# Gated linear attention's projection in three chunks of 512 columns instead of four of 384

## The chip, the core and the metric

The kernel runs on one core of a Trainium2 chip, as one program. TensorE (PE in the profile) multiplies matrices, VectorE (DVE), ScalarE (ACT) and GpSimd (POOL) work element by element, and SyncE (SP) issues nearly all DMA. Each engine takes its own instructions in order and waits on semaphores for the others. The metric is the device time of the whole program in microseconds (us), the median of several executions.

## What is computed

One layer of a decoder for 2048 prompt rows and 64 sample rows, in float32, cut to what the change is about:

```python
h = rms_norm(x, g_mix_pre)
proj = jnp.einsum('btd,de->bte', h, w_in)          # 1024 -> 512+128+128 | 256+256+512+512 | 16
q, k, v, gq, gk, gv, gr, glr = jnp.split(proj, points, axis=-1)
attn = swa_banded(rope(q), rope(k), v, sinks)       # window of 128, 8 heads
log_a = log_sigmoid(glr @ w_gk2 + b_gk) / 16
o, s_new = gla_chunked(gq, gk, gv, log_a, s_init)   # gated linear attention, 4 heads
gla_out = rms_norm(o, g_gla) * silu(gr)
mix = jnp.einsum('bte,ed->btd', concatenate([attn, gla_out]), w_out)
x = x + rms_norm(mix, g_mix_post)
# then a squared-ReLU MLP of width 4096 between two norms, and the residual
```

## The kernel before

Rows are cut into 17 tiles of 128 (tile 16, `NB`, holds the 64 sample rows). A float32 product is made of three: operands are split into a high part, rounded to float32r, and the rest, and `three` products (high by high, high by rest, rest by high) are summed in PSUM. A contraction over 1024 has 8 steps `k` of 128, so one tile by one chunk of columns takes 24 matmuls; for the sample rows, whose high and rest parts lie side by side as 128 rows, it takes 16.

The program has four parts: the attention (0 to some 290 us in the trace), the gated linear attention (to some 680 us), the output projection (to some 860 us) and the MLP.

The columns gq, gk, gv, gr (1536 of them) are the projection that is changed. `G_N` is the width of a chunk: four chunks of 384 columns. `projecting` multiplies one tile by a chunk into a PSUM bank of kind "a" (there are two), and then ScalarE copies the sum into `gp` (`gp_s` for the sample rows), scaled by the row's norm. These matmuls, `gproj` in the profile, are not made at one place: they are a generator, `fill`, from which other work takes a given number at a time while its own operands come from other engines. In the attention `A_FILL` says how many products are taken at which point of a unit, in the gated linear attention `G_FILL` does (34, 14, 16, 8 and 20 for each tile, 92 in all of the 96 that a tile needs). So PE has something to do while DVE and ACT make the next decays, keys and gates.

The weights of the chunks come from `w_in` by DMA (`load_gw`, tile `wg_raw`), are multiplied by the norm's gain and split (`split_gw`). The early ones (chunks 0 and 1) are loaded two a tile from tile 3 on and split by GpSimd and ACT, the late ones (chunks 2 and 3) after the attention's own weights `wa` are released, four in flight, split by ACT and DVE (`split_some`). Tiles 0 and 1 take their early chunks in the attention's last two tiles and the late ones in the part for the sample rows' attention. Then `products` projects the sample rows and tiles 2 to 15, one tile after the other.

When the last tile (15) is done with a chunk, the place of that chunk's weights is free. `load_wo` puts output weights there (`wo`; the split halves had been written to DRAM as `wo_d`), `place_mix` the first rows to be projected (`mt`), and `out_projecting` starts right behind the last `gproj`, still in the same `fill`. The order of PE, ACT and DVE in the attention is the order in which the code calls them (`InOrder`); elsewhere a scheduler orders the instructions, and it also orders SP's DMAs.

Of the kernel before, what the change touches and what calls it, by code (L numbers as in the profile page):

```python
# [21 lines left out]
P = 128  # L22
D = 1024
# [16 lines left out]
G_N = 384  # L40
# [15 lines left out]
G_EARLY, G_LATE = (0, 1), (2, 3)  # L56
# [16 lines left out]
G_GAINED = ((0, 2),)  # L73
G_NEXT = (NB, *range(2, NB))
G_ORDER = (0, 1, 2, 3)
# [3 lines left out]
WO_PARTS = ((), (0, 1, 2), (3, 4, 5), (6, 7))  # L79
# [73 lines left out]
def hybrid_step_kernel(ctx: ExitStack, tc: tile.TileContext, I, O):  # L153
# [83 lines left out]
    def load_raw(stg, k, c0, n, name, tag="w_raw", bufs=2):  # L237
# [13 lines left out]
    gw = {}  # L251

    def open_gw(chunks):
        p_ = open_pool(f"g_w{chunks[0]}", "right")
        for c in chunks:
            gw[c] = (p_, *(p_.tile([P, KT, G_N], F32R, tag=f"w{c}{u}", name=f"wg{c}_{u}") for u in range(2)))
        return p_
# [373 lines left out]
    def projecting(i, xT, chunks, act=nc.scalar):  # L631

        n, waiting = rows(i), []
        for c in chunks:
# [1764 lines left out]
```

## Time and profile before

| | |
|---|---|
| time, three runs | 2166.4, 2166.55 and 2170.19 us, median 2166.55 |
| span of the profiled execution | 2163.2 us, first to last instruction |
| instructions in it | 34238, of them 11799 matmuls |
| PE, ACT, DVE, POOL busy | 99%, 56%, 71%, 12% of the span |
| chain that ended last | PE 96%, DMA 1%, DVE 1%, ACT 1% |

The median is 3.35 us above the profiled span; this part lies around the first and the last instruction, and the change does not touch it. A matmul's end is modelled in this profile, and matmuls overlap: a PE that is busy all the time is not one that works at its peak, and the mean duration of a matmul is longer than the distance from one start to the next. Rates are therefore read from the chain and from starts in the timeline.

### The profile page before, as it was taken

The page shows a single profiled execution, that of the slowest core. Times are in us where ns is not written, and L with a number is a line of the kernel's source. Part 1 is how long each engine was busy: PE and PEld are TensorE (multiplying, and loading weights), DVE is VectorE, ACT ScalarE, POOL GpSimd, SP SyncE. Part 2 cuts the span into 40 slices and gives each one's busy share as a digit, 9 for nine tenths or more (in the row PEclk, how much of TensorE's full clock was granted, in tenths as well). Part 3 has the DMA queues.
Part 4 walks back from the last instruction along what each step waited for, and adds up shares of the span by engine and source line. Part 5 has one row for each costly group of instructions (what it writes and reads, how often), then busy time and mean ns, then how long its engine had stood idle before and what let it go on. Part 6 is the DMA issues. An engine that isn't in the chain of part 4 may idle for free.

```text
span 2163.2 us, 34238 instructions
## 1 busy us (share of the span) xinstructions
PE 2150.4 (99%) x11799; PEld 1864.7 (86%) x11799; DVE 1528.9 (71%) x3203; ACT 1220.9 (56%) x2625; POOL 258.5 (12%) x417
## 2 busy tenths in 40 slices
PE   9999999999999999999999999999999999999998
PEld 9999999999998888888888888887888888788887
DVE  7999868777875666988887555557766666555566
ACT  7999867566664444655555544344444445444454
POOL 4676501111111100000000000000000000000000
PEclk9999999999999999999999999999999999999999
DMA  7444241233437567777786777758544443766685
GB/s 242 159 142 149 98 117 46 75 108 123 147 124 276 188 217 227 250 259 273 259 275 219 261 244 223 230 181 266 177 170 161 151 160 125 247 203 195 195 262 186
DMA packets 241322, 411.54 MB, mean 190 GB/s; under 512 B 24876, under 2 KB 143132, under 8 KB 237036
## 3 DMA queue, kind: packets, MB, share of 16 engines
q1 hardware_dynamic: 240988, 409.08, 57.0%
q8 instruction: 93, 1.52, 0.3%
q14 instruction: 81, 0.66, 0.1%
q10 hardware_dynamic: 160, 0.27, 0.0%
HBM read 265.82 MB, written 143.99 MB: 189 GB/s over the span
## 4 chain that ended last, share of the span: by engine, by line
PE 96%; DMA 1%; DVE 1%; ACT 1%; issue 0%; DVEq 0%; SPq 0%; ACTq 0%
PE dn L142 26%; PE gproj L142 13%; PE uc L142 8%; PE uX L142 8%; PE out L1419 7%; PE proj L142 6%; PE ud L142 4%; PE ue L142 4%; PE ub L142 4%; PE sam L142 2%; PE dsam L142 1%; PE sc L142 1%; PE pT L142 1%; PE o L142 1%; PE av L142 1%; PE out L142 1%
## 5 line engine op out<-in xcount | busy, mean ns | idle before, releaser
L142 PE MATMUL dn<-o1t,o0s 128*128 128x512 f32 x892 | 348.2, 390 | 3.8 <-DVE o1t L229 3.8
L142 PE MATMUL dn<-o0t,o1s 128*128 128x512 f32 x892 | 347.8, 390 | 0.0
L142 PE MATMUL dn<-o0t,o0s 128*128 128x512 f32 x892 | 347.4, 389 | 0.3 <-DVE f L2071 0.3
L229 DVE TENSOR_TENSOR o1s<-rs,o0s 128x512 fp32r<-128x512 f32 x224 | 154.5, 691 | 223.0 <-ACT o0s L228 218.8
L228 ACT ACTIVATE o0s<-rs 128x512 fp32r<-128x512 f32 x224 | 141.2, 631 | 297.0 <-PE dn L142 262.0
L142 PE MATMUL gproj<-wg,gxh 128*128 128x384 f32 x1024 | 272.9, 342 | 0.0
L142 PEld LDWEIGHTS dn<-o1t,o0s 128*128 128x128 f32 x892 | 167.4, 188 | 41.1 <-DVE o1t L229 5.7
L142 PEld LDWEIGHTS dn<-o0t,o0s 128*128 128x128 f32 x892 | 167.5, 188 | 37.0 <-DVE f L2071 0.7
L142 ACT ACTIVATE st<-st 128x512 f32<-128x512 f32 x224 | 141.1, 630 | 100.3 <-DVE st L142 95.3
L142 PEld LDWEIGHTS dn<-o0t,o1s 128*128 128x128 f32 x892 | 167.4, 188 | 35.1
L142 PEld LDWEIGHTS gproj<-wg,gxh 128*128 128x128 f32 x1024 | 183.9, 188 | 3.5 <-issue 3.1
L142 PE MATMUL uc<-H,s 128*128 128x512 f32 x768 | 186.5, 391 | 0.0
L142 PE MATMUL gproj<-wg,gxl 128*128 128x384 f32 x576 | 185.8, 340 | 0.0
L142 PE MATMUL uX<-H,w 128*128 128x512 f32 x768 | 185.2, 390 | 0.0
L142 PEld LDWEIGHTS uX<-H,w 128*128 128x128 f32 x768 | 144.0, 188 | 30.3
L142 PEld LDWEIGHTS uc<-H,s 128*128 128x128 f32 x768 | 143.0, 188 | 30.6 <-ACT st L142 0.2
L1419 PE MATMUL out<-wo,mt 128*128 128x512 f32 x680 | 158.6, 392 | 0.0
L218 POOL TENSOR_TENSOR frs<-rs_v,half 128x1 f32<-128x1 f32 (+1 forms) x13 | 11.9, 925 | 1201.8 <-DVE rs_v L216 1201.8
L229 DVE TENSOR_TENSOR o1t<-rt,o0t 128x512 fp32r<-128x512 f32 x223 | 152.3, 685 | 3.8 <-ACT o0t L228 3.7
L1419 PEld LDWEIGHTS out<-wo,mt 128*128 128x128 f32 x680 | 126.5, 188 | 26.1
L228 ACT ACTIVATE o0t<-rt 128x512 fp32r<-128x512 f32 x223 | 137.8, 618 | 7.6 <-DMA rt<-t_d 4.9
L142 DVE TENSOR_TENSOR st<-st 128x512 f32<-128x512 f32 x160 | 110.7, 692 | 29.5 <-ACT st L142 25.2
(429 smaller groups left out, 4307.7 us busy)
## 6 DMA issues: line engine op xcount, KB each, us to landing
s_d<-st SPq DMA_DIRECT2D x32, 1792.0 KB, 8.5
rs<-s_d SPq DMA_DIRECT2D x224, 256.0 KB, 3.0
raw<-in_w_up SPq DMA_DIRECT2D x64, 512.0 KB, 4.6
rt<-t_d SPq DMA_DIRECT2D x128, 256.0 KB, 4.2
rt<-in_w_down SPq DMA_DIRECT2D x96, 256.0 KB, 3.2
t<-in_w_down SPq DMA_DIRECT2D x64, 256.0 KB, 3.7
t_d<-t SPq DMA_DIRECT2D x32, 512.0 KB, 5.7
h_d<-ht SPq DMA_DIRECT2D x8, 1280.0 KB, 7.6
```

What stands on the lines that cost most here:

```text
L142: ins = call(*a, **k)
L218: return nc.gpsimd.tensor_tensor(out, v[:n], e, op=ALU.pow)
L228: nc.scalar.activation(hi, src, AF.Copy)
L229: vector.tensor_tensor(lo, src, f32(hi), op=ALU.subtract)
L1419: te.matmul(banks[c], x, w[:, c * 512 : (c + 1) * 512], start=k + u == 0, stop=k == KT - 1 and u == len(products) - 1,)
```

## The change

The 1536 columns become three chunks of 512: chunk 0 is gq and gk, chunk 1 gv, chunk 2 gr. One tile by one chunk is still 24 matmuls. They are taken in the order 0, 2, 1 (`G_ORDER`). `fill` is now drawn by `pour`, in which a matmul of 512 columns counts as 4/3, so that the numbers of `A_FILL` and `G_FILL` mean the same columns as before.

Weights are kept in five pieces by chunk and step: chunk 0 in steps 0 to 5 and 6 to 7, chunk 1 in two halves, chunk 2 whole. Early are 12 pieces of 128x512 (chunk 0 and half of chunk 1), one a tile through one `w_raw` buffer instead of two a tile through two; late are the other 12, three in flight. Tiles 0 and 1 stop in the middle of chunk 1's sum and go on when the late half is there, so both "a" banks are held over that time. Output weights 0 to 3 take chunk 2's place, 4 and 5 that of chunk 1's first half, 6 and 7 that of its second; the first `mt` tiles and the gains lie in chunk 0's place.

```diff
-G_N = 384
+G_N = 512
...
-G_EARLY, G_LATE = (0, 1), (2, 3)
+G_EARLY, G_LATE = ((0, 0, 6), (0, 6, 8), (1, 0, 4)), ((1, 4, 8), (2, 0, 8))
...
+EARLY_WEIGHTS, LATE_WEIGHTS = ([(c, k) for c, k0, k1 in parts for k in range(k0, k1)] for parts in (G_EARLY, G_LATE))
...
-G_ORDER = (0, 1, 2, 3)
+G_ORDER = (0, 2, 1)
...
-WO_PARTS = ((), (0, 1, 2), (3, 4, 5), (6, 7))
+WO_PARTS = {(2, 0, KT): (0, 1, 2, 3), (1, 0, 4): (4, 5), (1, 4, KT): (6, 7)}
...
-    def load_raw(stg, k, c0, n, name, tag="w_raw", bufs=2):
+    def load_raw(stg, k, c0, n, name, tag="w_raw", bufs=1):
...
+    def open_gw(parts):
+        p_ = open_pool(f"g_w{parts[0][0]}", "right")
+        for c, k0, k1 in parts:
+            gw[c, k0] = p_
+            for u in range(2):
+                t = p_.tile([P, k1 - k0, G_N], F32R, tag=f"w{c}{k0}{u}", name=f"wg{c}{k0}_{u}")
+                gw_tiles[c, k0, u] = t
+                for k in range(k0, k1):
+                    wg[c, k, u] = t[:, k - k0, :]
         return p_
...
     def split_gw(c, k, raw):
-        if c in G_LATE or (c, k) in G_GAINED:
-            split_gained(gw[c][1][:, k, :], gw[c][2][:, k, :], raw, k)
+        hi, lo = (wg[c, k, u] for u in range(2))
+        if (c, k) in LATE_WEIGHTS or (c, k) in G_GAINED:
+            split_gained(hi, lo, raw, k)
             return
         with tc.issue_after(powers[3].ins):
             nc.gpsimd.tensor_tensor(raw, raw, gcol[:, k : k + 1].to_broadcast([P, G_N]), op=ALU.mult)
-        ac.activation(gw[c][1][:, k, :], raw, AF.Copy)
-        nc.gpsimd.tensor_tensor(gw[c][2][:, k, :], raw, f32(gw[c][1][:, k, :]), op=ALU.subtract)
+        ac.activation(hi, raw, AF.Copy)
+        nc.gpsimd.tensor_tensor(lo, raw, f32(hi), op=ALU.subtract)
...
-    def projecting(i, xT, chunks, act=nc.scalar):
-
-        n, waiting = rows(i), []
-        for c in chunks:
-            p_ = bank([P, 512], "a", f"gproj_{i}_{c}")
-            _, wh, wl = gw[c]
-            products = ((xT[1], wh), (xT[1], wl)) if i == NB else ((xT[0], wh), (xT[0], wl), (xT[1], wh))
-            for k in range(KT):
+    late_copies_g, g_banks = [], {}
+
+    def projecting(i, xT, pieces, act=nc.scalar):
+
+        n = rows(i)
+        for c, k0, k1 in pieces:
+            if k0 == 0:
+                g_banks[i, c] = bank([P, 512], "a", f"gproj_{i}_{c}")
+            p_ = g_banks[i, c]
+            for k in range(k0, k1):
+                wh, wl = (wg[c, k, u] for u in range(2))
+                products = ((xT[1], wh), (xT[1], wl)) if i == NB else ((xT[0], wh), (xT[0], wl), (xT[1], wh))
                 for u, (x, w) in enumerate(products):
-                    te.matmul(
-                        p_[:, :G_N], x[:, k, :], w[:, k, :],
-                        start=k + u == 0, stop=k == KT - 1 and u == len(products) - 1,
-                    )
-                    yield
-                    if waiting and (k, u) == (0, 2):
-                        act.activation(*waiting.pop(), scale=rstd_all[:n, i : i + 1])
+                    te.matmul(p_, x[:, k, :], w, start=k + u == 0, stop=k == KT - 1 and u == len(products) - 1)
+                    yield 4 / 3
+                    if late_copies_g and (k, u) == (0, 2):
+                        late_copies_g.pop()()
+            if k1 < KT:
+                continue
             if i not in gps:
                 gps[i] = gp_pool.tile([P, G_W], F32, tag="gp", name=f"gp_{i}", bufs=2)
             out = gps[i][:n, c * G_N : (c + 1) * G_N]
-            src = folded(out, p_[:, :G_N]) if i == NB else p_[:, :G_N]
-            if act is ac and (i, c) == (0, chunks[0]):
-                waiting.append((out, src, AF.Copy))
+            src = folded(out, p_) if i == NB else p_
+            copy = partial(act.activation, out, src, AF.Copy, scale=rstd_all[:n, i : i + 1])
+            if act is ac and (i, c) == (0, 0):
+                late_copies_g.append(copy)
             else:
-                act.activation(out, src, AF.Copy, scale=rstd_all[:n, i : i + 1])
+                copy()
...
+    def pour(n):
+
+        poured[0] += n
+        while poured[0] > 0.5:
+            cost = next(fill, 0)
+            if cost == 0:
+                break
+            poured[0] -= cost or 1
...
-            for n in range(4):
-                stage = ("w_raw", 2) if n % 2 else ("x", 2)
+            for n in range(3):
+                stage = ("w_raw", 1) if n == 1 else ("x", 2)
                 weights.append((*load_gw(*late.popleft(), *stage), stage))
         elif i >= 3:
             with tc.issue_after(third.ins):
-                for _ in range(min(2, len(early))):
+                if early:
                     weights.append((*load_gw(*early.popleft()), None))
...
-            fill = chain(fill, projecting(t, gxTs[t], G_EARLY, ac))
+            fill = chain(fill, projecting(t, gxTs[t], [(0, 0, KT)], ac))
+            if t:
+                fill = chain(fill, *(projecting(a, gxTs[a], [(1, 0, 4)], ac) for a in G_FIRST))
...
-                split_some(2)
+                split_some(1)
...
-    fill = chain(fill, *(projecting(t, gxTs[t], G_LATE, ac) for t in G_FIRST))
+    fill = chain(fill, *(projecting(t, gxTs[t], [part], ac) for part in G_LATE for t in G_FIRST))
...
-        split_some(4)
+        split_some(3)
...
-    def load_wo(ks, c):
-
-        parts = [gw[c][0].tile([P, 3, D], F32R, tag=f"w{c}{u}", name=f"wo{u}_{c}") for u in range(2)]
-        if len(ks) == 2:
-            late_mix.extend(t[:, 2, :512].rearrange("p (h t) -> p h t", h=4) for t in parts)
-            g_mix.extend(f32(t[:, 2, 512:]) for t in parts)
+    def place_late():
+
+        parts = [gw[0, 6].tile([P, 2, 512], F32R, tag=f"w06{u}", name=f"late{u}") for u in range(2)]
+        late_mix.extend(t[:, 0].rearrange("p (h t) -> p h t", h=4) for t in parts)
+        g_mix.extend(f32(t[:, 1]) for t in parts)
+
+    def load_wo(c, k0, ks):
+
+        parts = [gw[c, k0].tile([P, len(ks), D], F32R, tag=f"w{c}{k0}{u}", name=f"wo{u}_{c}{k0}") for u in range(2)]
         wo.update((k, [t[:, n, :] for t in parts]) for n, k in enumerate(ks))
         load_wo_half(ks, 0)
...
-            for c, ks in zip(G_ORDER, WO_PARTS):
-                columns = projecting(i, xT[i], (c,))
-                if after is None and c == G_ORDER[2]:
-                    yield from islice(columns, 10)
+            if after is not None:
+                yield from projecting(i, xT[i], [(c, 0, KT) for c in G_ORDER])
+                continue
+            for c, k0, k1 in ((0, 0, KT), *WO_PARTS):
+                columns = projecting(i, xT[i], [(c, k0, k1)])
+                if c == G_ORDER[1]:
+                    yield from islice(columns, 4)
+                    placed = [place_mix(j) for j in B_ORDER[:2]]
+                    place_late()
+                    yield from islice(columns, 15)
                     mixes.update((m[0], split_mix(*m, put)) for m in placed)
                 yield from columns
-                if after is None:
-                    load_wo(ks, c)
-                    if c == G_ORDER[1]:
-                        placed = [place_mix(j) for j in B_ORDER[:2]]
-                    if c == G_ORDER[3]:
-                        load_wo_half(range(KT), 1)
-                        for h, t in enumerate(g_mix):
-                            loaded = nc.sync.dma_start(t, gain_d[h : h + 1].rearrange("a d -> (a d)").partition_broadcast(P))
-                        raw = ss.tile([P, KT, P], F32, tag="part1", name="mt_raw", bufs=2)
-                        i = B_ORDER[2]
-                        with tc.issue_after(loaded.ins):
-                            nc.sync.dma_start(raw, mix_d[i])
+                if c:
+                    load_wo(c, k0, WO_PARTS[c, k0, k1])
+            load_wo_half(range(KT), 1)
+            for h, t in enumerate(g_mix):
+                loaded = nc.sync.dma_start(t, gain_d[h : h + 1].rearrange("a d -> (a d)").partition_broadcast(P))
+            raw = ss.tile([P, KT, P], F32, tag="part1", name="mt_raw", bufs=2)
+            i = B_ORDER[2]
+            with tc.issue_after(loaded.ins):
+                nc.sync.dma_start(raw, mix_d[i])
```

On PE, near the end of the projection (tile 15; `gproj_2` and the like are sums of a chunk, `wg` its weights, `gxh` and `gxl` the rows' high part and rest, `o` and `gqk` belong to the gated linear attention), before:

```order
L142 MATMUL o_9152<-S_4976,qd_4991 128x128
L142 MATMUL o_9152<-gp_8765,AT 128x128
L142 MATMUL gqk_9175<-ident,gp_9026 128x128 x4
L142 MATMUL gproj_2_9079<-wg_1_4412,gxh_8674 128x384
L142 MATMUL gproj_2_9079<-wg_0_4411,gxl_8675 128x384
L142 MATMUL gproj_3_9194<-wg_0_4413,gxh_8674 128x384
L142 MATMUL gproj_3_9194<-wg_1_4414,gxh_8674 128x384
L142 MATMUL gproj_3_9194<-wg_0_4413,gxl_8675 128x384
```

and with the change:

```order
L144 MATMUL o_8693<-S_4900,qd_4915 128x128
L144 MATMUL o_8693<-gp_8354,AT 128x128
L144 MATMUL gqk_8716<-ident,gp_8589 128x128 x4
L144 MATMUL gproj_1_8687<-wg_0_192,gxl_8257 128x512
L144 MATMUL gproj_1_8687<-wg_0_192,gxh_8256 128x512
L144 MATMUL gproj_1_8687<-wg_1_193,gxh_8256 128x512
```

Behind `gqk` chunk 3 of 24 matmuls was still to come, and two of chunk 2; now 19 matmuls of chunk 1 are, and chunk 2, whose place takes output weights 0 to 3, has ended ahead of `o`.

On SP, the loads of the first mixed rows (`mt`), of the output weights (`wo`, by `u` and chunk; `wo_d0` is step 0) and of the gains (`gain_d`), before:

```order
L1205 DMA mix_d13_76<-mo0_4986 128x512
L1379 DMA mt_4_9077<-mix_d4_67 128x1024
L1379 DMA mt_0_9075<-mix_d0_63 128x1024
L1461 DMA wo1_1_9068<-wo_d0_147 128x512
L1461 DMA wo0_1_9067<-wo_d0_147 128x512
L1461 DMA wo0_1_9067<-wo_d1_148 128x512
L1461 DMA wo1_1_9068<-wo_d1_148 128x512
L1461 DMA wo0_1_9067<-wo_d2_149 128x512
L1461 DMA wo1_1_9068<-wo_d2_149 128x512
L1461 DMA wo0_1_9067<-wo_d0_147 128x512
L1461 DMA wo1_1_9068<-wo_d0_147 128x512
L1461 DMA wo0_1_9067<-wo_d1_148 128x512
```

and with the change:

```order
L1230 DMA mix_d13_76<-mo0_4910 128x512
L1403 DMA mt_4_8598<-mix_d4_67 128x1024
L1403 DMA mt_0_8596<-mix_d0_63 128x1024
L1512 DMA late0_8600<-gain_d_158 128x512
L1512 DMA late1_8601<-gain_d_158 128x512
L1516 DMA mt_raw_8774<-mix_d1_64 128x1024
L1488 DMA wo1_20_8678<-wo_d0_147 128x512
L1488 DMA wo0_20_8677<-wo_d0_147 128x512
L1488 DMA wo0_20_8677<-wo_d1_148 128x512
L1488 DMA wo1_20_8678<-wo_d1_148 128x512
L1488 DMA wo0_20_8677<-wo_d2_149 128x512
L1488 DMA wo1_20_8678<-wo_d2_149 128x512
```

The gains and the third tile's rows (`mt_raw`) stood behind all 32 loads of `wo` and now stand ahead of them, and the second halves of steps 0 to 2 (the 7th to 12th load of `wo`) now come behind all 16 first halves.

## Rows read from the trace of the kernel before

**Rows 1.** Page, part 1: busy us (share of the span) xinstructions of each engine.

```profile
PE 2150.4 (99%) x11799; PEld 1864.7 (86%) x11799; DVE 1528.9 (71%) x3203; ACT 1220.9 (56%) x2625; POOL 258.5 (12%) x417
```

**Rows 2.** PE waits, 27 to 660 us: us in total, times, longest.

```profile
PE pT L142 <- DVE s L142: 0.4, 1, 0.4
PE pT L142 <- ACT s L142: 0.2, 1, 0.2
```

**Rows 3.** Groups of instructions by line and shape, whole span.

```profile
L142 PE MATMUL gproj<-wg,gxh 128*128 128x384 f32 x1024 | 272.9, 342 | 0.0
...
L142 PE MATMUL gproj<-wg,gxl 128*128 128x384 f32 x576 | 185.8, 340 | 0.0
```

**Rows 4.** Chain that ended last, 500 to 700 us: start us, us, what.

```profile
632.53 5.90 PE gproj L142 x34
639.05 5.26 PE gproj L142 x30
648.12 3.67 PE gproj L142 x20
...
660.83 6.86 PE out L142 x30
671.98 4.75 PE out L142 x20
...
685.80 11.84 PE out L1419 x52
```

**Rows 5.** Timeline of PE around the last tile: start us, us, what.

```profile
644.28 0.60 PE L142 MATMUL gproj<-wg,gxh 128*128 128x384 f32 x2
...
645.85 0.45 PE L142 MATMUL gl<-XQ,kt 128*64 128x64 f32 x8
...
651.63 0.38 PE L142 MATMUL o<-S,qd 128*128 128x128 f32 x2
...
653.77 0.42 PE L142 MATMUL gproj<-wg,gxh 128*128 128x384 f32 x1
...
658.37 2.02 PE L142 MATMUL out<-wo,mt 128*128 128x512 f32 x8
...
667.66 2.11 PE L142 MATMUL out<-wo,mt 128*128 128x512 f32 x8
669.70 0.45 PE L142 MATMUL gl<-XQ,kt 128*64 128x64 f32 x8
```

**Rows 6.** Stretches in the attention: busy us (instructions) of each engine, clock, DMA.

```profile
130.00:180.00 50.00, 50.00 (x347) 48.81 (x346) 45.62 (x155) 46.42 (x125) 37.30 (x63) 1.00 0.41 139
180.00:230.00 50.00, 50.00 (x344) 48.92 (x343) 45.73 (x157) 44.85 (x122) 28.06 (x54) 1.00 0.41 142
```

**Rows 7.** Tile wg_raw: ns min/median/max of its instructions; landing of its loads.

```profile
L267 POOL TENSOR_TENSOR wg_raw<-wg_raw,gcol x15: 826/827/828, 49.8 to 183.5; 128x384 f32<-128x384 f32 x15
L142 ACT ACTIVATE wg<-wg_raw x15: 507/512/527, 81.1 to 193.8; 128x384 fp32r<-128x384 f32 x15
...
DMA to landing us min/median/max: 2.4/2.4/3.3
```

**Rows 8.** Groups by line and shape, 250 to 660 us: copies out of PSUM.

```profile
L654 ACT ACTIVATE gp<-gproj,rstd_all 128x384 f32<-128x384 f32 x56 | 32.2, 574 | 11.4 <-PE gproj L142 10.7
```

**Rows 9.** Stretches around 375 us (columns as in rows 6).

```profile
370.00:375.00 5.00, 5.00 (x37) 4.66 (x36) 4.07 (x13) 3.80 (x12) 1.04 (x1) 1.00 0.00 1
375.00:380.00 5.00, 5.00 (x71) 4.54 (x70) 2.61 (x6) 1.71 (x6) 0.00 (x0) 0.66 0.51 178
```

**Rows 10.** Timeline of the DMA queue on SP, 640 to 690 us.

```profile
641.04 0.80 SPq L1379 DMA_DIRECT2D mt<-mix_d  x2
645.43 22.81 SPq L1461 DMA_DIRECT2D wo<-wo_d  x32
```

**Rows 11.** Tile wo: its loads from issue to landing.

```profile
DMA to landing us min/median/max: 5.3/6.1/6.8
```

**Rows 12.** All waits from 260 to 320 us: us in total, times, longest.

```profile
DVE mo_s L142 <- DMA wg_raw<-in_w_in: 1.1, 1, 1.1
```

More of the change, by code (lines that the diff above doesn't have):

```diff
@@ L2 @@
 from contextlib import ExitStack, nullcontext
+from functools import partial
 from itertools import chain, cycle, islice
@@ L249, in hybrid_step_kernel @@
     gcol = cpool.tile([P, KT], F32, name="gcol")
-    gw = {}
-    def open_gw(chunks):
-        p_ = open_pool(f"g_w{chunks[0]}", "right")
-        for c in chunks:
-            gw[c] = (p_, *(p_.tile([P, KT, G_N], F32R, tag=f"w{c}{u}", name=f"wg{c}_{u}") for u in range(2)))
+    gw, gw_tiles, wg = {}, {}, {}
+    def open_gw(parts):
[7 more added lines that the diff above has]
+                    wg[c, k, u] = t[:, k - k0, :]
         return p_
@@ L823, in start @@
                 norms[k // 2]()
-        xTs[2] = [t[:, :, :P] for t in gw[G_EARLY[1]][1:]]
+        xTs[2] = [gw_tiles[1, 0, u].rearrange("p k (a b) -> p (k a) b", b=P)[:, :KT] for u in range(2)]
         x2 = [*x_half(2, 0), *x_half(2, 1, "e")]
@@ L849, in start @@
         ac.activation(sinkp, pj, AF.Copy)
-        run(fill, A_LEAD)
+        pour(A_LEAD)
         return left
+    poured = [0.0]
+    def pour(n):
[5 more added lines that the diff above has]
+            poured[0] -= cost or 1
     def split_some(n):
@@ L859, in split_some @@
                 weights.append((*load_gw(*late.popleft(), *stage), stage))
-    early, late = (deque((c, k) for c in cs for k in range(KT)) for cs in (G_EARLY, G_LATE))
+    early, late = deque(EARLY_WEIGHTS), deque(LATE_WEIGHTS)
     weights = deque()
@@ L930, in hybrid_step_kernel @@
             if u == 1 and i < NB - 1:
-                split_some(2)
+                split_some(1)
             later = next(queue)
             next(later)
-            run(fill, A_FILL[u][0])
+            pour(A_FILL[u][0])
             next(behind, None)
@@ L937, in hybrid_step_kernel @@
                 next(behind, None)
-            run(fill, A_FILL[u][1])
+            pour(A_FILL[u][1])
             if u == 0:
@@ L946, in hybrid_step_kernel @@
             do(u, "X")
-            run(fill, A_FILL[u][2])
+            pour(A_FILL[u][2])
             if u:
@@ L988, in hybrid_step_kernel @@
         later = next(queue, None)
-        run(fill, 3 * (1 - n % 2))
+        pour(3 * (1 - n % 2))
         next(now)
@@ L993, in hybrid_step_kernel @@
             cached["k", 1] = load_cache("k", 1)
-        run(fill, 10 - 3 * (1 - n % 2))
+        pour(10 - 3 * (1 - n % 2))
         if n == 2:
@@ L1004, in hybrid_step_kernel @@
             next(later)
-        run(fill, 13)
+        pour(13)
         next(now)
         next(behind, None)
-        split_some(4)
+        split_some(3)
         if ahead:
@@ L1013, in hybrid_step_kernel @@
     next(behind)
-    run(fill, 8)
+    pour(8)
     run(behind)
@@ L1214, in gla @@
     def gla(i, gp, og=iter(())):
-        assert {(i, 0), (i, 1)} <= projected
+        assert (i, 0) in projected
         before, after = pre.pop(i)
@@ L1241, in gla @@
         yield G_FILL[1] - 3 * (i == 1), True
-        assert {(i, c) for c in range(4)} <= projected
+        assert {(i, c) for c in range(3)} <= projected
         sg = gate(i, gp, P)
@@ L1313, in gla_sample @@
         yield from decays(i, NS, s_before, "b")
-        assert {(i, c) for c in range(4)} <= projected
+        assert {(i, c) for c in range(3)} <= projected
         sg = gate(i, gp, NS)
@@ L1373, in place_mix @@
         n = rows(i)
-        p_, c = gw[G_ORDER[0]][0], G_ORDER[0]
-        m = p_.tile([P, 3, KT, P], F32R, tag=f"w{c}{B_ORDER.index(i) % 2}", name=f"mt_{i}")
+        m = gw[0, 0].tile([P, 3, KT, P], F32R, tag=f"w00{B_ORDER.index(i) % 2}", name=f"mt_{i}")
         ks = KT // 2 if i == NB - 1 else KT
@@ L1492, in products @@
         yield from first
-        m = gw[G_ORDER[0]][0].tile([P, 3, KT, P], F32R, tag=f"w{G_ORDER[0]}0", name=f"mt_{i}")
+        m = gw[0, 0].tile([P, 3, KT, P], F32R, tag="w000", name=f"mt_{i}")
         mixes[i] = split_mix(i, m, KT, raw)
@@ L1536, in hybrid_step_kernel @@
         for n, free in chain.from_iterable(parts):
-            deque(islice(fill, n // 2), 0)
+            pour(n // 2)
             if free:
                 next(side, None)
-            deque(islice(fill, n - n // 2), 0)
+            pour(n - n // 2)
         if i == 0:
```

1 line of the change is left out of this document (removed).

## Prediction

> **What bounds the kernel now.** I read the page first: PE is busy all the time [rows 1], which by itself says little, since a matmul's end is modelled. So I asked next what PE waits for between 27 and 660 us, the stretch that holds nearly all of the attention and the whole projection. The answer has two lines and 0.6 us in all [rows 2]: no engine and no DMA holds PE up there. The chain that ended last then shows, piece by piece, that the way to the end goes through the `gproj` matmuls themselves [rows 4]. So a matmul taken out of `gproj` shortens the program by what it costs from one start to the next, as long as nothing else becomes late. The mean duration (342 ns, [rows 3]) is not that cost: the chain has 34 of them in 5.90 us, 173.5 ns each, and for 512 columns 52 `out` in 11.84 us, 227.7 ns each.
>
> **The matmuls.** 1024 + 576 = 1600 `gproj` [rows 3] become 1200: 16 tiles by 3 chunks by 24, and 48 for the sample rows. Every four of 384 columns become three of 512. In a long run that is 4 x 173.5 = 694.0 ns against 3 x 227.7 = 683.1 ns, 10.9 ns less, and 400 times that is 4.4 us: the upper bound of the saving. The columns are the same, and what is saved is only the part of a matmul that does not grow with them. In a warm array at the granted 2.4 GHz, 384 columns take 160.0 ns and 512 take 213.3, so this part is 13.5 and 14.4 ns.
>
> The Trainium skill has a smaller one (TensorE: Matmul & The Clock Gate, the section "Wait — 56ns, not 53.3ns?"): start to start is the columns over 2.4 GHz and a fixed 2.5 ns. By that page the 400 matmuls would be worth an estimated 1.0 us. The chain's 13.5 ns do not agree, and the sum goes by them.
>
> But `gproj` comes in short runs between other matmuls, and the first one or two of a run are dearer. So I price the four runs of a tile one by one, each against a run of 512-column `out` matmuls behind the same or a like neighbour, shortened by 227.7 ns per matmul too many:
>
> - 34, now 25.5: 5.90 us; 30 `out` take 6.86, less 4.5 x 0.2277 = 5.84. Saving 0.06 [rows 4].
> - 30, now 22.5: 5.26 us; 6.86 less 7.5 x 0.2277 = 5.15. Saving 0.11 [rows 4].
> - 20, now 15: 3.67 us; 20 `out` take 4.75, less 5 x 0.2277 = 3.61. Saving 0.06 [rows 4].
> - 8, now 6: 645.85 - 644.28 = 1.57 us; 8 `out` take 669.70 - 667.66 = 2.04, less 2 x 0.2277 = 1.58. Saving -0.01 [rows 5].
>
> Together 0.22 us for 92 of a tile's 96 matmuls, 0.23 for all, and 14 tiles make 3.2 us. The 256 that are left (tiles 0 and 1, sample rows) lie in short runs among attention and sample matmuls: at the rate of the run of 8 they lose 0.3, at a tile's rate they save 0.6, and I take nothing. **Sum: 3.2 us**; lower bound nothing, upper 4.4.
>
> **What lies beside it.** *The copies out of PSUM*: ACT takes 574 ns for 128x384 [rows 8]; 48 wider ones in place of 64 are less work for ACT, which PE doesn't wait for, so nothing. Each bank now has 24 matmuls of 0.2277 us = 5.5 us to be emptied in, not 4.2. That tiles 0 and 1 hold both "a" banks costs nothing while no other work asks for that kind; the attention's own projection, which does, is over by then.
>
> *Early weights*: one piece a tile over twelve tiles, not two over eight. The multiplication on POOL takes 0.83 us, so some 1.1 for 512 columns, ACT's copy 0.51, some 0.7, a load lands in 2.4 to 3.3 us [rows 7]. With one buffer POOL's multiplication waits for a load that could only be issued when the piece before was split; behind it on POOL stand the copies of the keys, for which the next tile's scores wait on PE. It is hidden as before, since POOL is busy 37 of 50 us with the splits and 28 in the stretch where they end, and PE issues 347 and 344 matmuls in these two stretches [rows 6]: with or without splits it gets the same done. If that cover were gone, a load and a multiplication, up to 4.4 us a tile, would come free of it; I take nothing.
>
> *Late weights*: three larger loads in flight instead of four. ACT and DVE take the splits in order, and the sample rows' softmax stands behind them. Before, the one wait for such a load is 1.1 us on DVE [rows 12], which PE does not feel; I take nothing, with 1.1 us for the other end.
>
> *Output weights*: this is the place where the change takes slack away. First `wo` load at 645.43 [rows 10], first `out` at 658.37 [rows 5]: 12.9 us ahead. With the change the loads wait for the end of chunk 2, which is 24 matmuls (5.5 us) and the `o` block (653.77 - 651.63 = 2.1 us, [rows 5]) ahead of the first `out`: 7.6 us. From first issue to last landing it took 22.81 us of issuing [rows 10] and 6.1 of landing [rows 11], 28.9, with SP's pauses for weights still in use. So the last half lands some 21.3 us behind the first `out`. It is needed 69 matmuls (15.7 us) and the blocks between them (669.70 to 671.98 is 2.3; `o` 2.1; two groups of transposes, some 0.5) later: 20.6 us. That is a wait of 0.7 us at worst, and none if SP pauses less, since the last loads no longer wait for a place that comes late. I take nothing. The `mt`, gain and `mt_raw` loads ahead of them, 2 MB, go out when chunk 0 is done, some 8 us earlier, and are needed no sooner than before.
>
> **Forecast**: 2166.55 - 3.2 = **2163.35 us**. By span: 2163.2 to 2160.0. Within 0.2% (4.3 us) of before is about what a measurement of this kernel can't tell from no change.
>
> **Rivals.**
>
> *All of the upper bound, or a clock that stays up* (faster). From 375 to 380 us the granted clock is 0.66 in the mean [rows 9], that is half speed, 1.2 GHz, for two thirds of the stretch, right behind the sample rows' smallest matmuls (`s_oi`, `s_oe`); (1 - 0.66) x 5 = 1.7 us are lost there at most. The runs around it change from 4 matmuls of 384 to 3 of 512. If the clock stays up, 3.2 + 1.7 = 4.9 us are saved; if short runs are as good as long ones, 4.4. Time about 2161.9. Against it: the busy time around those matmuls is the same to a hundredth. As well it could fall a second time, which leaves 1.5 us.
>
> *Nothing is saved*: a 512-column matmul costs 4/3 of one with 384, 231.3 ns, as the run of 8 has it (2.04 to 1.57 is 1.30, [rows 5]) and as it would be if time went by columns alone. Then 2166.55, and up to 1.6 less. The skill's page above, with its 2.5 ns, lies here. For it: the runs get shorter still. Against it: three of the four pairs.
>
> *Output weights come late* (slower). If the loads took 37 us instead of 28.9, because other traffic slows them, the last one would land 29.4 us behind the first `out`, 8.8 us late: 2163.35 + 8.8 = 2172.2. The gain is gone when they take over 31.4 us, and the kernel is slower by 4.3 us from 35.7 on, a quarter more than now. Against it: the first half of them has to be there only at 1.4 us a step, and DMA elsewhere in that stretch does the same as before.
>
> **How the numbers follow.** Saving 1.6 to 4.3 us: 0.45. Nothing to 1.6 us: 0.17. More than 4.3 us: 0.28. Late weights of either kind, slower: 0.10. So faster by over 0.2% 0.28, within 0.2% 0.62, slower 0.10. The range has to leave out 2 in 10: 2161.0 (the upper bound and a clock that stays up leave a little below it) to 2167.2 (nothing saved, and a wait of 0.7).
>
> **What would show it.** Right: the chain after still goes through `gproj`; 1200 of them; runs of 25 or 26, 22 or 23, 15 and 6 in the times above; no wait of PE on `wo`. The copies out of PSUM at about 0.6 us, 48 of them. Wrong: long runs at 231 ns (the second rival), a PE wait behind the first 60 `out` (the third), a second stretch with a clock under 0.9, or a PE wait at `sc` or `pT` in tiles 11 to 14, where POOL now splits.

## The result and the profile after

The changed kernel takes 2170.6 us (median; 2168.41 to 2173.3, 20 runs), the kernel before on the same chip 2166.24 us (2162.45 to 2170.19, 20 runs). The ratio is 1.0021 (95% interval 1.0015 to 1.0027): slower by 0.2%, where 2163.35 us was forecast, and above the top of the forecast's range (2167.2). The profiled span is 2167.2 us, 4.0 more than before. In every run whose span is on record the time is 1.7 to 1.9 us above the span; of the 3.35 us between the median and the span before, only this part lies around the first and the last instruction, and the rest is the difference between one execution and another. The page has 400 matmuls fewer, and PE is again busy for 99% of the span:

```profile
PE 2149.4 (99%) x11399; PEld 1810.7 (84%) x11399; DVE 1532.7 (71%) x3198; ACT 1215.2 (56%) x2599; POOL 257.4 (12%) x409
```

To see where the time went I paired the matmuls of the two traces and took, at pairs that stand at the same place of the program, how much later the one of after starts. The growth of this shift per stretch, in us; the other two columns are of experiments told below (e1 mends only POOL's order, e7 three places):

| stretch (us) | part | after | e1 | e7 |
|---|---|---|---|---|
| 0 to 86 | first tiles | -0.45 | -0.39 | -0.14 |
| 86 to 119 | attention, tiles 3 to 5 | **+4.19** | +0.88 | +0.89 |
| 119 to 261 | attention | -0.05 | -0.04 | -0.05 |
| 261 to 310 | sample rows, late weights | **+1.71** | +1.54 | +1.21 |
| 310 to 374 | tiles 0, 1, 2 of the projection | -0.22 | -0.14 | -0.31 |
| 374 to 386 | around the clock's fall | -1.50 | -1.50 | +0.07 |
| 386 to 698 | tiles 2 to 15, first `out` | **-1.85** | -1.86 | -1.86 |
| 698 to 859 | output projection | 0 | 0 | 0 |
| 859 to 870 | first tiles of the MLP | **+1.32** | +1.36 | +0.01 |
| 870 to 1847 | MLP | -1.01 | -1.71 | +0.17 |
| 1847 to 1913 | MLP | +1.61 | +1.63 | +1.59 |
| all | | +3.75 | -0.23 | +1.58 |

The projection itself did gain, by less than forecast. The loss lies in three places that the forecast priced at nothing or didn't have.

PE's waits between 27 and 660 us, 0.6 us in two lines before [rows 2], are now 4.8 in six (us in total, times, longest):

```profile
PE proj L144 <- ACT qk L144: 1.9, 1, 1.9
PE av L144 <- DVE pl L144: 1.5, 3, 0.8
PE ssc L144 <- ACT kc L144: 0.6, 1, 0.6
PE pT L144 <- ACT s L144: 0.4, 2, 0.2
PE sav L144 <- DVE spc L144: 0.2, 1, 0.2
PE pT L144 <- DVE s L144: 0.2, 1, 0.2
```

The longest of them is in tile 4 of the attention. PE's row there, ACT's rows that it waits for, and POOL's rows that ACT waits for, from the timelines (start us, us, what, and in brackets the idle time before it and what ended it):

```profile
102.56 0.44 PE L144 MATMUL proj<-wa_hi,xh 128*128 128x392 f32 x1 [1.91 <-ACT qk L144]
...
100.38 0.63 ACT L144 ACTIVATE wg<-wg_raw 128x512 fp32r<-128x512 f32 x1 [3.79 <-POOL wg_raw L275]
101.03 0.38 ACT L144 ACTIVATE rest<-av 64x256 f32<-64x256 f32 x1
101.44 0.60 ACT L144 ACTIVATE xh<-xT 128x512 fp32r<-128x512 f32 x1
101.93 0.58 ACT L144 ACTIVATE qk<-proj,rstd_all 128x392 f32<-128x392 f32 x1
...
99.17 0.19 POOL L502 COPY s<-sink 128x2 f32<-128x2 f32 x1 [2.15 <-PE pT L144]
99.31 1.04 POOL L275 TENSOR_TENSOR wg_raw<-wg_raw,gcol 128x512 f32<-128x512 f32 x1
101.09 1.26 POOL L277 TENSOR_TENSOR wg<-wg_raw,wg 128x512 fp32r<-128x512 f32 x1 [0.74 <-ACT wg L144]
```

Read from the bottom up: the 0.19 us copy of the sinks stands first in POOL's order and waits 2.15 us for PE to be done with a score tile. The weights' multiplication behind it could have gone earlier: its load was issued at 82.64 and landed 2.7 us later. ACT stands still for 3.79 us until the multiplication ends, and behind that row on ACT are `rest`, `xh` and the copy `qk` for which PE waits. Before, the same rows stand in the other order, the multiplication ahead of the copy (timeline of POOL before):

```profile
97.48 0.83 POOL L267 TENSOR_TENSOR wg_raw<-wg_raw,gcol 128x384 f32<-128x384 f32 x1
98.95 1.00 POOL L269 TENSOR_TENSOR wg<-wg_raw,wg 128x384 fp32r<-128x384 f32 x1 [0.64 <-ACT wg L142]
100.35 0.19 POOL L494 COPY s<-sink 128x2 f32<-128x2 f32 x1 [0.40 <-PE pT L142]
```

The chain around the last tile is the same as before in kind, through `gproj` and then `out` (start us, us, what); each run of `gproj` stands for one in [rows 4]:

```profile
634.67 5.74 PE gproj L144 x25
641.03 5.34 PE gproj L144 x23
650.17 3.65 PE gproj L144 x15
...
662.66 6.86 PE out L144 x30
```

### The profile page after: what moved, and what is told of

Read it like the earlier page. It is cut to its first block, busy times and chain, and to the rows that moved or that the text cites. A ratio compares the mean times of both kernels' runs of the same rounds, so it can differ in the third digit from the quotient of the medians.

```text
span 2167.2 us, 33375 instructions
## 1 busy us (share of the span) xinstructions
PE 2149.4 (99%) x11399; PEld 1810.7 (84%) x11399; DVE 1532.7 (71%) x3198; ACT 1215.2 (56%) x2599; POOL 257.4 (12%) x409
## 4 chain that ended last, share of the span: by engine, by line
PE 94%; ACT 2%; DVE 2%; DMA 1%; issue 1%; POOL 0%; DVEq 0%; ACTq 0%; POOLq 0%
PE dn L144 26%; PE gproj L144 12%; PE uc L144 8%; PE uX L144 8%; PE out L1443 7%; PE proj L144 6%; PE ud L144 4%; PE ue L144 4%; PE ub L144 4%; PE sam L144 2%; PE dsam L144 1%; PE sc L144 1%; PE pT L144 1%; PE o L144 1%; PE av L144 1%; PE out L144 1%
## 5 line engine op out<-in xcount | busy, mean ns | idle before, releaser
L144 PE MATMUL gproj<-wg,gxh 128*128 128x512 f32 x768 | 242.2, 395 | 0.0
L144 PE MATMUL gproj<-wg,gxl 128*128 128x512 f32 x432 | 168.3, 407 | 0.0
L144 PEld LDWEIGHTS gproj<-wg,gxh 128*128 128x128 f32 x768 | 143.1, 188 | 28.1 <-issue 0.3
```

The source lines that it names most:

```text
L144: ins = call(*a, **k)
```

## Experiments

Each time stands beside the kernel before, run on the same chip in the same batch; the ratio and its interval are those on record, not the quotient of the two medians. The expectations count from the 2170.6 us of the first batch, in which the kernel before took 2166.24. In the later batches it took 0.8 to 1.3 us less, so the ratios are what to compare: the changed kernel has 1.0021.

**e1, POOL's order.** The gain's multiplication goes ahead of the copy of the sinks in that one unit; nothing else differs from the changed kernel.

```diff
+            gained.append(nc.gpsimd.tensor_tensor(raw, raw, gcol...))
...
-        nc.gpsimd.tensor_copy(s[:, :, nk : nk + 1], sink...)
+        with tc.issue_after(gained[1].ins) if (i, r, jj) == (5, 0, 0) else nullcontext():
+            nc.gpsimd.tensor_copy(s[:, :, nk : nk + 1], sink...)
```

> The changed kernel with two neighbouring rows of POOL exchanged in tile 4 of the attention: the gain multiplication of the weight piece now stands ahead of the copy of the sink, as it did before the change; every other row of every engine stands as in the changed kernel. Theory: ACT's copy of that piece waits for POOL's multiplication, POOL's multiplication waits behind a copy that waits for PE's transposes, and PE in the end waits for ACT; the 4.2 us that the trace shows between 96 and 122 us are this, so 2170.6 - 4.2 = 2166.4 us, and no stretch with a granted clock of 0.89 at 95 to 110 us. Rival, one buffer for the pieces and a load that comes late: the load is not moved, so 2170.6 us.

Measured: 2166.69 us (11 runs) beside 2164.95 (33 runs), ratio 1.0004 (0.9994 to 1.0013). POOL's and ACT's timelines at the same place:

```profile
97.04 1.04 POOL L277 TENSOR_TENSOR wg_raw<-wg_raw,gcol 128x512 f32<-128x512 f32 x1
99.21 0.19 POOL L505 COPY s<-sink 128x2 f32<-128x2 f32 x1 [1.13 <-ACT rest L144]
...
98.11 0.63 ACT L144 ACTIVATE wg<-wg_raw 128x512 fp32r<-128x512 f32 x1 [1.48 <-POOL wg_raw L277]
```

The multiplication runs 2.3 us earlier, PE's wait of 1.9 is gone, and the shift of this stretch falls from 4.19 to 0.88 us. Two rows in another order are most of the loss. What stays has two parts. PE waits 0.8 us at `av` for DVE's `pl`, as in after, where before waits 0.4 at `pT` for DVE (first line of [rows 2]); by the pairing this exchange costs 0.25 us. Another 0.6 us are lost from 116 to 118 us, behind the first piece that ACT and DVE split with the gain in it; the kernel before splits its one early piece of this kind a tile earlier, at 97 us.

The 4.19 us are more than the 1.9 of the wait. The stretch from 95 to 110 us of after and then of e1 (us, busy time and instructions of PE, PEld, DVE, ACT and POOL, granted clock, DMA share, GB/s) shows a second part:

```profile
95.00:110.00 15.00, 12.26 (x71) 11.41 (x71) 9.59 (x34) 9.98 (x29) 5.33 (x13) 0.89 0.42 134
```

```profile
95.00:110.00 15.00, 14.22 (x94) 13.33 (x93) 12.56 (x44) 12.71 (x35) 8.46 (x15) 1.00 0.44 145
```

After PE's pause the granted clock fell to its lower level (1.2 GHz) for a part of the stretch: (1 - 0.89) x 15 = 1.65 us at most. The sum 0.88 + 1.9 + 1.65 is 4.4, beside 4.19. The fall does not always come: in e3, which has the same pause, the clock is 1.00 and the shift 3.19 us. Of the five profiles with this pause (after, e2, e3, e5, e6) four show the fall there, of the nine without it none. The recorded executions say the same: the mean granted clock of a kernel's executions is 0.9972 to 0.9976 for these five and 0.9983 to 0.9990 for before, e1, e4, e7, e8 and e9, and a thousandth of the span is 2.2 us. So the fall is part of what POOL's order costs in the median too.

**e2, four late pieces in flight** in place of three, the fourth in a place that the attention's `qk` had; only SP's order of loads changes.

```diff
-            for n in range(3):
-                stage = ("w_raw", 1) if n == 1 else ("x", 2)
+            for n in range(4):
+                stage = ("w_raw", 1) if n == 1 else ("qk", 2) if n == 3 else ("x", 2)
```

> The changed kernel with four late weight pieces in flight in place of three (a free place of the same size is used); only the order of loads on SP changes. Theory: the 2.0 us that ACT waits for a load at 296 us delay the cached keys' copy behind it, for which PE waits 0.6 us; with four in flight that goes, 2170.6 - 0.6 = 2170.0 us. Rival: the 1.7 us lost between 262 and 316 us come from wider splits on ACT and DVE, for which PE waits elsewhere; then no change, 2170.6 us.

Measured: 2170.43 us beside 2164.95, 1.0019 (1.001 to 1.0028). In the changed kernel ACT's split waits for such a load and PE for ACT behind it (timeline of ACT, then PE's waits from 262 to 330 us):

```profile
298.14 0.73 ACT L144 ACTIVATE wg<-wg_raw,gcol 128x512 fp32r<-128x512 f32 x1 [2.04 <-DMA wg_raw<-in_w_in]
...
PE av L144 <- DVE pl L144: 0.7, 2, 0.5
PE ssc L144 <- ACT kc L144: 0.6, 1, 0.6
PE sav L144 <- DVE spc L144: 0.2, 1, 0.2
PE pT L144 <- ACT s L144: 0.2, 1, 0.2
```

The four waits make 1.7 us, the +1.71 of the table. With a fourth load `ssc`'s 0.6 is gone, the others stay, and the stretch costs 1.21. That is too small a part for the median to show, and the trace does not show it for this edit alone: in e3 and e5, with three loads in flight as in after, ACT's wait for the load is 1.6 and 0.6 us in place of 2.0, PE does not wait at `ssc` either, and the stretch costs 1.32 and 1.23. How late the load is differs between executions. PE felt it in three of five profiles with three loads in flight (after, e1, e6) and in none of eight with four.

**e3, other places for the output weights.** My theory was that the +1.32 us at the MLP's opening came from the squared features lying over the weights of rows 4 and 5.

```diff
-WO_PARTS = {(2, 0, KT): (0, 1, 2, 3), (1, 0, 4): (4, 5), (1, 4, KT): (6, 7)}
+WO_PARTS = {(1, 0, 4): (0, 1), (2, 0, KT): (2, 3, 4, 5), (1, 4, KT): (6, 7)}
```

> The changed kernel with the output weights in other places: rows 0 and 1 of them where 4 and 5 were, 2 to 5 where 0 to 3 were. Theory: the first split features of the MLP lie over the weights that the last output matmuls read; with rows 4 and 5 there they wait for PE until 42 of the last 48 matmuls are done, with rows 0 and 1 until 30, so the 1.2 us that the trace shows behind 860 us come back: 2169.4 us. Rival: the wait there comes from the order of ACT's rows or from loads, and nothing comes back: 2170.6 us.

Measured: 2169.92 us beside 2164.95, 1.002 (1.0012 to 1.0029), and PE's wait at `uX` is 1.1 us as in the changed kernel: the theory fell. The timeline of ACT says what it is instead; first after (with PE's wait at `uX` ahead of it), then e3, then before:

```profile
PE uX L144 <- ACT st L144: 1.1, 1, 1.1
...
858.40 2.01 ACT L144 ACTIVATE H<-hraw 128x1024 fp32r<-128x1024 f32 x2 [2.12 <-PE out L1443]
861.12 1.06 ACT L144 ACTIVATE s<-t 128x1024 fp32r<-128x1024 f32 x1 [0.71 <-PE out L1443]
...
866.08 0.61 ACT L144 ACTIVATE st<-uX 128x512 f32<-128x512 f32 x1
```

```profile
855.91 2.01 ACT L144 ACTIVATE H<-hraw 128x1024 fp32r<-128x1024 f32 x2
860.87 1.06 ACT L144 ACTIVATE s<-t 128x1024 fp32r<-128x1024 f32 x1 [2.95 <-PE out L1443]
```

```profile
855.65 1.06 ACT L142 ACTIVATE s<-t 128x1024 fp32r<-128x1024 f32 x1 [0.25 <-DVE t L142]
```

In e3 the features `H` no longer wait, but the row behind them, `s<-t`, does, until the last `out` is done. My reading, which e5 and e6 test: its tile lies where the late half of the last tile's rows (`late`) was put, which that `out` reads. Before, `s<-t` ran at 855.65 us and not at 861.12, behind no matmul.

**e4, e1 to e3 together.**

> The three edits of the runs before in one kernel. Theory, the three losses lie behind each other on PE and add up: 2170.6 - 4.2 - 0.6 - 1.2 = 2164.6 us, that is 1.6 us less than before the change, which is then what the wider matmuls and the clock that stays up at 376 us are worth. Rival, time won early is given back later at waits for loads or for the next stage: 2166 us or more.

Measured: 2167.01 us beside 2164.95, 1.0007 (0.9998 to 1.0016), no better than e1 and not the 2164.6 expected: e3 is worth nothing, and what e2 is worth is too small to see.

**e5, another place for the late half.** It and the gains go into a fourth row of chunk 2's tiles, and `wo` row 0 to where they lay.

```diff
+WO_FIRST, WO_PARTS = (0,), {(2, 0, KT): (1, 2, 3), (1, 0, 4): (4, 5), (1, 4, KT): (6, 7)}
...
+        rows_ = len(ks) + (c == 2)
...
+            late_mix.extend(t[:, 3, :512]... for t in parts)
...
-                    place_late()
+                    load_wo(0, 6, WO_FIRST)
```

> The changed kernel with the gains and the late half of the last tile's mix out of the two small tiles of chunk 0 (where the change had put them) and into the fourth row of chunk 2's tiles; output weight row 0 goes into the small tiles instead. Output weights 4 and 5 stay under the first split features of the MLP. Theory, formed after the run with other weight rows moved nothing: ACT's first split sum of the MLP lies over the late half of the mix, which the very last output matmul reads; behind it on ACT stand five rows and the copy for which PE waits 1.1 us behind 860 us. With that place free the split sum starts at 860.2 in place of 861.1 us, and PE gets 0.9 of 1.3 us back: 2169.7 us by median. Rival, the features over weights 4 and 5 hold ACT: nothing, 2170.6 us.

Measured: 2169.55 us beside 2165.41 (35 runs), 1.0019 (1.0011 to 1.0028). The wait at `uX` falls from 1.1 to 0.2 us, another of 0.4 appears at `uc` 32 us later, and the shift of the stretch from 859 to 870 us is +0.5 in place of +1.3.

**e6, this and, as in e3, earlier rows under `H`**, so that neither `H` nor `s<-t` lies over what the last `out` reads (the diff is against e5).

```diff
-WO_FIRST, WO_PARTS = (0,), {(2, 0, KT): (1, 2, 3), (1, 0, 4): (4, 5), (1, 4, KT): (6, 7)}
+WO_FIRST, WO_PARTS = (0,), {(1, 0, 4): (1, 2), (2, 0, KT): (3, 4, 5), (1, 4, KT): (6, 7)}
```

> As the run before, and output weight rows 1 and 2 in place of 4 and 5 under the first split features. ACT's order there is then that of the kernel before the change, the features ahead of the copies. Theory: the wait of PE behind 860 us is gone altogether, 2170.6 - 1.3 = 2169.3 us, and no wait of PE at uX in the trace. Rival, loads are what is late there: the wait stays.

Measured: 2168.95 us beside 2165.41, 1.0017 (1.0008 to 1.0025). The wait is gone altogether and the shift is 0. ACT's row in e6 (timeline) is again released by DVE and by no matmul, as before:

```profile
858.15 1.06 ACT L144 ACTIVATE s<-t 128x1024 fp32r<-128x1024 f32 x1 [0.25 <-DVE t L144]
```

So the places, both of them together, cost the 1.3 us. In the median that is at the edge of what can be told (1.0017 and 1.0021 with overlapping intervals); the trace shows it.

**e7, e1, e2 and e6 together.**

> The exchange of two rows on POOL, four late pieces in flight, and the places of the run before together. Theory: 2166.7 (with POOL's rows exchanged) - 1.3 - 0.5 = 2164.9 us by the median of the earlier runs, the time of the kernel before the change within 0.1%: what is left of the saving of the wider matmuls, some 1.9 us in the projection of the tiles, is eaten by dearer short runs and wider splits around the sample rows. Rival, my forecast's sum, 3.2 us less than before: 2161.8 us.

Measured: 2165.35 us (12 runs) beside 2165.41, ratio 0.9994 (0.9985 to 1.0003). With the three places mended the change is worth nothing that can be measured, and no loss either. The mean granted clock of the executions is 0.9987 in both. PE's waits from 27 to 660 us are then:

```profile
PE av L144 <- DVE pl L144: 1.5, 3, 0.8
PE pT L144 <- ACT s L144: 0.4, 2, 0.2
PE sav L144 <- DVE spc L144: 0.2, 1, 0.2
```

In the last attention tile, splits on ACT and DVE stand ahead of the rows that PE waits for (`pl` of the softmax); they take 0.71 and 0.75 us for 512 columns with the gain in them, where they took 0.61 and 0.62 for 384. That these cause the two later waits at `av` is read from the order, and e9 tests it in part. The longest one, 0.8 in tile 4, has no split on DVE ahead of it; there DVE waits 1.15 us for ACT's `rest`, which stands behind ACT's copy of the weights, and that copy 1.48 us for POOL's multiplication. No run takes this wait away. By the table 0.89 us are lost in tiles 3 to 5 and 1.21 at the sample rows, 2.1 together. The projection's gain is 1.86 + 0.31 = 2.2 us. One pays for the other.

**e8, e7 with the products in another order** (in tiles 2 and on): all eight high by high, then high by rest, then rest by high. In the steady part `gproj` starts come 226, 229 and 232 ns apart in turn, 229.0 in the mean (the expectations say 229.2), `out` 226.7; was it the operands that alternate?

```diff
-            for k in range(k0, k1):
-                for u, (x, w) in enumerate(products):
+            steps = [(k, u) for k in range(k0, k1) for u in range(len(plan))]
+            if i > 1:
+                steps.sort(key=lambda s: s[1])
```

> As the run before, with the three products of a chunk one behind the other for all eight rows of weights (in tiles 2 and on), not row by row; as many matmuls, the same columns. In the trace of the changed kernel a gproj matmul takes 229.2 ns start to start in a long run, in a repeating 226, 229, 232, and an out matmul 226.7. Theory, the repeating three is the three products (two of them with the same stationary tile): grouped, a run goes at another steady rate, and at 226.7 it would be 1200 times 2.5 ns, 3.0 us less, 2161.9 us. Rival, it is something of the place of the operands or of the other engines' work: still 229.2 ns, 2164.9 us.

Measured: 2164.75 us beside 2165.41, 0.9997 (0.9988 to 1.0005), and the same three distances. The order is not the cause: a run of 25 in the chain takes 5.74 us in e7 and in e8.

**e9, e7 with the low parts of the first four late pieces on POOL** in place of DVE, which takes work from DVE ahead of `pl`.

```diff
+        if (c, k) in LATE_WEIGHTS[:4]:
+            ac.activation(hi, raw, AF.Copy, scale=gcol[:, k : k + 1])
+            nc.gpsimd.tensor_tensor(raw, raw, gcol..., op=ALU.mult)
+            nc.gpsimd.tensor_tensor(lo, raw, f32(hi), op=ALU.subtract)
+            return
```

> The kernel with all three repairs (POOL's rows, four late pieces, places), and the low parts of the four late pieces that are split during the last attention tile made by POOL in two steps, not by DVE in one; POOL has no other work there. Theory: the 1.5 us that PE waits at av for pl between 276 and 290 us, in every run since the change and not before it, come from the 0.75 us splits that stand ahead of pl on DVE; without them the waits go and the time falls by 1.0 to 1.5 us, to 2164.1 us by median. Rival, pl is late by ACT's copies (0.62 us each, as many as before): no change, 2165.3 us.

Measured: 2165.65 us beside 2165.09 (15 runs), 1.0002 (0.9993 to 1.0011). PE's waits, 27 to 660 us:

```profile
PE av L144 <- DVE pl L144: 1.1, 2, 0.8
PE sav L144 <- DVE spc L144: 0.5, 2, 0.3
...
PE spt L144 <- DVE ss L144: 0.3, 1, 0.3
```

One `av` wait is gone and one is half as long. By the pairing with before, 0.4 us are gained up to 276 us of its trace and 1.0 up to 285, so DVE's splits are what `pl` stood behind; then waits at `sav` and `spt` take nearly all of it back by 290, and the stretch costs 1.10 us in place of 1.21.

**e10, e11, e12, e7 with an unused 256, 512 or 1024 bytes a partition** ahead of the transposed rows, so that the stationary operands of `gproj` lie elsewhere; one run each.

```diff
+    pad = kp.tile([P, 64], F32, name="pad")
+    nc.gpsimd.memset(pad, 0.0)
```

> The kernel with all three repairs and an unused 256 B a partition ahead of the transposed inputs, so that these lie 256 B further against the weights; nothing else differs. Theory: the steady 229.2 ns of a gproj matmul, against 226.7 of an out matmul of the same shape, hang on where the operands lie, and in the MLP too runs of one shape go at 226.7, 230 or 233.5 ns; so the long runs change to another of these values. Rival, the place does not matter: 25 gproj still go from gqk to ogT in 5.82 us.

> As the run before with 512 B. By the theory another rate than 229.2 ns, at this or at one of the other two shifts; by the rival 5.82 us for 25 again.

> As the two runs before with 1024 B. By the theory another rate than 229.2 ns, at this or at one of the other two shifts; by the rival 5.82 us for 25 again.

Measured: 2165.27, 2165.75 and 2166.77 us beside 2165.09. From the first of 25 `gproj` to the next block it is 5.82 us in each, 229.0 ns a matmul in the steady part. Shifts of that kind on that side are not the cause; others were not tried.

## Why the prediction was wrong, step by step

In the forecast's own terms, the 3.2 us saved by the matmuls became about 2.1, and two terms put at nothing and one that it did not have became losses of 4.19, 1.71 and 1.32 us.

**The step that failed: early weights.** The prediction said of them "It is hidden as before" and took nothing. It had found the chain's first half: POOL's multiplication waits, and copies stand behind it. It looked only behind the multiplication on POOL, at the keys. It missed what stands ahead of it there, the sinks' copy that waits for PE, and that ACT waits for the multiplication with `qk` behind it. Nor was the cover what it was said to be: that PE issues as many matmuls with as without splits [rows 6] shows that the kernel before has no such wait, and not how little is missing for one. The load that it feared was on time. The uncovered price that it named, up to 4.4 us a tile, was for a late load in front of a multiplication; that 4.19 us were lost, in one tile and another way, is a coincidence of size. The price got no place in the range, and the one chance of a loss, 0.10, was for weights that land late. The forecast also said that a wait at `sc` or `pT` in tiles 11 to 14 would prove it wrong; the wait came in tile 4, at `proj`. The sign that did come true is another one it named, a second stretch with a clock under 0.9: 0.89 from 95 to 110 us and 0.68 from 1855 to 1860. e1 shows the step: 4.19 us become 0.88.

**Matmuls: the mechanism was right, the term too large.** 3.2 us were forecast for 14 tiles; 1.85 were measured from 386 us on and 0.22 in the stretch ahead of it, so about 2.1. The groups, whole span (mean ns behind the comma), show the 1200 that were to be seen:

```profile
L144 PE MATMUL gproj<-wg,gxh 128*128 128x512 f32 x768 | 242.2, 395 | 0.0
...
L144 PE MATMUL gproj<-wg,gxl 128*128 128x512 f32 x432 | 168.3, 407 | 0.0
```

The runs of the chain, start to the next block: 34 to 25, 5.985 to 5.820; 30 to 23, 5.262 to 5.335; 20 to 15, 3.580 to 3.554; 8 to 6, 1.569 to 1.561 us. Together 92 matmuls in 16.396 us become 69 in 16.270, 0.13 us a tile where 0.22 was forecast; over the ten whole tiles from 410 to 632 us of before it is 0.15 in the mean, 0.12 to 0.13 in most. The reason is the rate: `gproj` of 512 columns takes 229.0 ns in the steady part, and the forecast took 227.7 from `out`. Four of 173.3 are 693.3, three of 229.0 are 687.0: 6.3 ns less and not the 10.9 of the prediction. That one row of another matmul stood for this one was the mistake; in the chain of before, `uX` and `uc`, twelve of 512 columns each, stand side by side and differ by 7 ns a matmul:

```profile
1561.26 2.72 PE uX L142 x12
1563.98 2.80 PE uc L142 x12
```

Of the Trainium skill's rule on this (TensorE: Matmul & The Clock Gate, "Wait — 56ns, not 53.3ns?": a fixed 2.5 ns beside the columns) the trace does not agree in the rate, 229.0 ns where it gives 215.7. The gain by it was an estimated 1.0 us, and the trace has about 2.1: the rule says less than was measured, the prediction more.

**Late weights** were put at nothing, with 1.1 us for the other end; they cost 1.71. Up to 0.6 of it is the wait at `ssc` for a late load, which three loads in flight allow and do not bring each time (e2, e3, e5). The other 1.1 to 1.3 come in every profile of the change; that the wider splits on ACT and DVE make them is shown for the part up to 285 us (e9) and argued for the rest. The prediction read the wait before [rows 12] as one that PE does not feel, and did not ask how little more it takes for PE to feel it.

**The MLP's opening** was not in the list at all. The prediction followed the new places up to their loads and not to the tiles that later lie over them. e6 takes the 1.3 us away.

**The clock.** The rival with a clock that stays up came true in the profile of after, and is worth nothing. Stretches of before, of after and of e7:

```profile
1850.00:1855.00 5.00, 3.12 (x14) 2.58 (x15) 4.85 (x8) 3.56 (x7) 0.00 (x0) 1.00 0.77 278
```

```profile
375.00:380.00 5.00, 5.00 (x33) 4.16 (x31) 3.91 (x14) 3.68 (x13) 0.44 (x1) 1.00 0.17 55
1855.00:1860.00 5.00, 5.00 (x17) 3.93 (x16) 3.26 (x7) 1.97 (x4) 0.00 (x0) 0.68 0.88 300
```

```profile
375.00:380.00 5.00, 5.00 (x63) 4.52 (x64) 2.71 (x7) 2.75 (x9) 0.00 (x0) 0.83 0.54 172
1850.00:1855.00 5.00, 3.13 (x9) 2.52 (x10) 4.82 (x8) 3.07 (x6) 0.00 (x0) 0.78 0.81 279
```

After keeps 1.00 near 376 us, where before had 0.66 [rows 9], and falls near 1855, where before stayed up; the -1.50 and the +1.61 of the table cancel. e7 falls at both, which makes its span longer than before at the same median time. Over all fourteen profiles the fall between 375 and 385 us is there in seven and that between 1850 and 1860 in eight, with no edit that goes with either. Nor does a pause of PE decide it: ahead of the second place PE waits 2.1 us at `dn` in all fourteen, and at the first it is busy throughout. A single profile should not be asked whether a change saves such a fall.

**What was right.** *Output weights*: the first load went out at 652.5 us, 7.7 to 7.9 ahead of the first `out` (forecast 7.6), and the last landed 18.2 us behind it (forecast 21.3 at worst, needed at 20.6). PE did not wait for them. Tile `wo`, its loads on the queue and from issue to landing, answers to [rows 10, 11]:

```profile
L1488 SPq DMA_DIRECT2D wo<-wo_d x32: 319/320/431, 652.5 to 673.0; - x32
...
DMA to landing us min/median/max: 5.1/5.4/5.9
```

*Prices of the wider rows*: POOL's multiplication was forecast at 1.1 us and took 1.04, ACT's copy at 0.7 and took 0.62 (tile `wg_raw`, 60 to 340 us; ns min, median, max), both a little less than [rows 7] in proportion. The copies out of PSUM take 685 ns (forecast about 0.6 us), 574 before [rows 8], and PE does not wait for them.

```profile
L144 ACT ACTIVATE wg<-wg_raw x11: 616/620/631, 80.6 to 260.8; 128x512 fp32r<-128x512 f32 x11
...
L275 POOL TENSOR_TENSOR wg_raw<-wg_raw,gcol x10: 1039/1040/1042, 99.3 to 249.8; 128x512 f32<-128x512 f32 x10
```

**What stays open.** Why `gproj` takes 229.0 ns and `out` 226.7 for the same columns; that `uc` in the MLP changes its rate from one run of twelve to the next, in the same program, says that it need not be the instruction. The wait of 0.8 at `av` in tile 4, and the waits at `spt` and `sav` that come up in e9, no run takes away. And the stretch from 870 to 1847 us, which the change does not touch, has a shift of -1.71 to +1.65 us over the thirteen profiles beside before; PE's waits there, at `dn` for DVE, differ from one profile to the next, and I did not look further. So a sum over the whole span, as the +3.75, is good to some 2 us only, and the reading rests on the stretches.

## What to carry to other kernels

When a step is moved, write down for each engine that executes a part of it the rows that now stand ahead of and behind it, the engines that only pass it on too: here the two rows that cost 3.3 us could be read from the order on POOL before any run. A new place in memory is followed to the next tile that lies over it, not only to its own load. A saving of a few ns a matmul needs a price from several runs of that shape, and has to be set against the waits, here of 0.2 to 1.9 us each, that the wider pieces bring elsewhere.

## What the runs showed of the hardware

Matmuls of 128x512 run steadily at different distances: 226.7 ns in `out` and in the MLP's `uX`, 229.0 in `gproj` (three distances in turn). `uc` changes from one run of twelve to the next: 233.3 and 226.7 ns in turn from 1545 us on, 229.0 and 226.7 in turn before 1200 us, alike in before, after and e7. The order of the products (e8) and shifts of the stationary operands by 256 to 1024 bytes (e10 to e12) left the 229.0 as it was.

The granted clock fell to 1.2 GHz at the same two places of the program in some profiles and not in others, for 1.5 to 1.6 us of lost time each by the pairing of before and after: near 376 us with PE busy throughout (seven of fourteen profiles), near 1852 us behind a wait of PE of 2.1 us that all fourteen have (eight of them). A third place is behind PE's wait of 1.9 us at 101 us, in four profiles of the five that have this wait.
